# Modulation per row tile, its products in column groups, and a separate bank for the last half block

## Chip, cores and metric

The kernel runs on one core of a Trainium2 chip. The metric is the device time of one execution in microseconds (us). The engines are named as the profile names them: PE (TensorE) multiplies matrices, with PEld as its weight loads; DVE (VectorE), ACT (ScalarE) and POOL (GpSimd) work on elements; SP (SyncE) issues transfers.

## What is computed

One layer of a two-branch mixer over 256 latent and 256 context tokens, with 2048 features. The part that the change touches at the front is the modulation (`adaLN`) ahead of the input projection, and at the back the last normalisation:

```
shift, scale, gate = jnp.split(sc @ w_ada[l] + b_ada[l], 3, axis=-1)
hx = _rmsnorm(x, g_pre[l]) * (1.0 + scale[:, None]) + shift[:, None]
zx = hx @ w_in[l]
...
out = _rmsnorm(_mix_out(...), g_post[l])
x = x + gate[:, None] * out
```

The context stream does the same with `c_ctx`. `w_ada` is 2048 by 6144, and two thirds of it (32 MiB) are read for shift and scale. The rest of the layer (a depthwise convolution, a state space scan in both directions, a gated MLP, the output projection) is not changed.

## The kernel before

All weights are fp32. A weight piece is split into a rounded part `hi` (ACT) and a remainder `lo` (DVE), and every product of the projections is three matmuls, `hi` with `hhi`, `hi` with `hlo`, `lo` with `hhi`, where `hhi[k]` and `hlo[k]` are the two parts of the normalised and modulated input of feature tile k (lines 136 to 140).

**The first stage (lines 229 to 382)** walks the 16 feature tiles ("row tiles") as 16 rows. Row kt multiplies tile kt of the input with the part of the weights that belongs to it, `wst[kt]`: first the dt columns (`psdt`, lines 362 and 363, two matmuls), then seven column tiles psx0 to psx6, three matmuls each; psx3 and psx6 use 256 columns, the others 512. All sums stay in PSUM until row 15. In this stage the order on PE, DVE, ACT and POOL is the program's (`manual_schedule`, line 231), and `row_steps(kt)` writes out each row's steps.

Before row kt can run, its input tile must be shifted and scaled. The shift and scale come from `w_ada`, which arrives as 32 chunks of 1 MiB. `ada_mm(ci)` (line 205) multiplies one chunk: the two condition vectors are the weights (32 columns wide, two of them used), the chunk streams past, and four column groups of the array work side by side, each on another 32 feature columns. A unit is the accumulation that serves one or two tiles: units 0 and 1 serve tiles 0 and 1 (two chunks each, 64 columns per matmul), the seven others serve two tiles each (four chunks, 128 columns per matmul). When a unit is full, `ada_fin(u)` transposes it on DVE (line 222) and writes scale `ha` and shift `hb` with two ACT operations per tile (lines 224 and 226). Then `make_h(kt)` makes the tile: DVE scales it (line 307, two halves), ACT adds the shift and rounds to `hhi` (line 310, two halves), DVE makes `hlo` (line 312, two halves). `split_st(kt)` makes the weights' parts: ACT casts the whole row (line 299), DVE makes the dt remainder (line 300) and `lo` (line 301).

In rows 0 to 2 the two chunks stand apart, between products; in row 0 two more, chunks 4 and 5, stand at the end. In rows 3 to 13 the two chunks stand side by side. The tile of the next row is made in the middle of a row, once the unit that it needs is full: after chunk 3 for tile 1, after chunk 7 for tiles 2 and 3.

Transfers are issued on SP in program order: the input `xT` (4 MiB), then chunk 0, `wst[0]`, chunks 1 to 3, `wst[1]`, chunks 4 and 5, and in row kt chunks 2kt+6 and 2kt+7 and `wst[kt+2]`. Six chunks have room.

While PE waits for tile 0 it runs dummy matmuls (`warm`, line 254).

**The last stage (lines 1055 to 1149).** The output projection leaves eight banks, token tile tk = 0, 1 by column block b = 0 to 3. `ofinish` adds the last quarter of the sum. The last block (1, 3) is done as two halves of 256 columns in the same bank. For each block `o_sum` scales the bank and adds the other branch (DVE, line 1108), squares it with a row sum (ACT, line 1111), and multiplies by the gate (DVE, line 1114). Then per token tile: reduce, square root (ACT, line 1119), reciprocal (line 1122), and `o_out`: scale, add the input (DVE, line 1127) and send 256 KB out, on SP's and ACT's queues by turns. DVE's order is the program's here, the other engines' is the planner's.

Of the kernel before, what the change touches and what calls it, by code (L numbers as in the profile page):

```python
# [15 lines left out]
P = 128  # L16
D = 2048
# [8 lines left out]
WST = 64 + NST * P  # L26

# [14 lines left out]
def tile_hybrid_ssd_mlp(  # L42
# [252 lines left out]
    def split_st(kt):  # L295
        raw = wraw[kt]
        hi = wp["spl"].tile([P, WST + 64], F32R, tag="hi", name=f"hi_st{kt}")
        lo = wp["spl"].tile([P, WST - 64], F32R, tag="lo", name=f"lo_st{kt}")
        nc.scalar.copy(hi[:, 64:], raw)
        nc.vector.tensor_tensor(hi[:, 0:64], raw[:, 0:64], hi[:, 64:P].bitcast(F32), op=ALU.subtract)  # L300
        nc.vector.tensor_tensor(lo, raw[:, 64:], hi[:, P:].bitcast(F32), op=ALU.subtract)
        return hi, lo
# [20 lines left out]
    sp0 = {}  # L323

    def row_steps(kt):
# [3 lines left out]
        nxt = [("h", kt + 1), ("s", kt + 1)]  # L329
# [892 lines left out]
```

## Time and profile before

| | us |
|---|---|
| time, median of 3 runs (994.25 to 994.62) | 994.32 |
| the profiled execution's own time | 995.11 |
| its span | 993.4 |
| PE busy in the span | 976.1 |
| DVE busy | 623.0 |
| ACT busy | 493.6 |
| granted clock, mean share of full speed | 0.998 |

The page shows the span in 40 slices of 24.8 us. PE is at 9 tenths or more in all of them but the first and the last. The DMA engines are at 9 in the first four slices and between 1 and 8 after. Busy time on PE is modelled and consecutive matmuls overlap in it, so prices below are taken from one start to the next start, not from durations.

### The profile page before, as it was taken

The page shows a single profiled execution, that of the slowest core. Times are in us where ns is not written, and L with a number is a line of the kernel's source. Part 1 is how long each engine was busy: PE and PEld are TensorE (multiplying, and loading weights), DVE is VectorE, ACT ScalarE, POOL GpSimd, SP SyncE. Part 2 cuts the span into 40 slices and gives each one's busy share as a digit, 9 for nine tenths or more (in the row PEclk, how much of TensorE's full clock was granted, in tenths as well). Part 3 has the DMA queues.
Part 4 walks back from the last instruction along what each step waited for, and adds up shares of the span by engine and source line. Part 5 has one row for each costly group of instructions (what it writes and reads, how often), then busy time and mean ns, then how long its engine had stood idle before and what let it go on. Part 6 is the DMA issues. An engine that isn't in the chain of part 4 may idle for free.

```text
span 993.4 us, 14183 instructions
## 1 busy us (share of the span) xinstructions
PE 976.1 (98%) x5636; PEld 791.3 (80%) x5636; DVE 623.0 (63%) x944; ACT 493.6 (50%) x759; POOL 111.7 (11%) x162
## 2 busy tenths in 40 slices
PE   8999999999999999999999999999999999999996
PEld 3788888878787878787888878887888888888885
DVE  4345478877877666656667766666555564445636
ACT  4233348566655554545445334454565563346522
POOL 0000002423453221224000000000000000000000
PEclk9999999999999999999999999999999999999999
DMA  9999744233314324145778768774445445556722
GB/s 377 421 416 419 296 184 170 85 128 128 128 48 164 127 91 165 43 152 210 294 304 288 265 244 314 267 289 171 170 176 202 173 169 212 183 198 236 272 86 84
DMA packets 31554, 207.28 MB, mean 209 GB/s; under 512 B 4080, under 2 KB 4208, under 8 KB 7808
## 3 DMA queue, kind: packets, MB, share of 16 engines
q1 hardware_dynamic: 28656, 192.52, 51.3%
q0 software_dynamic: 2112, 12.65, 3.7%
q10 hardware_dynamic: 720, 1.20, 0.3%
q8 instruction: 44, 0.72, 0.3%
q14 instruction: 22, 0.18, 0.0%
HBM read 204.20 MB, written 2.16 MB: 208 GB/s over the span
## 4 chain that ended last, share of the span: by engine, by line
PE 80%; issue 8%; DMA 6%; DVE 2%; ACT 1%; POOL 1%; SPq 0%; DVEq 0%; POOLq 0%; ACTq 0%
PE psx L138 10%; PE psx L140 10%; PE psx L139 10%; PE pa L1027 8%; PE pa L1028 8%; PE pa L1029 8%; PE pm L1076 3%; PE pm L1075 3%; PE pm L1074 3%; PE psada L215 3%; PE pq L1075 2%; PE pq L1076 2%; PE pq L1074 2%; DMA ada<-in_wada_dram 2%; PE psc L697 1%
## 5 line engine op out<-in xcount | busy, mean ns | idle before, releaser
L82 DVE TENSOR_TENSOR lo_w<-w,hi_w 128x1024 fp32r<-128x1024 f32 x173 | 210.6, 1224 | 141.7 <-ACT hi_w L81 141.7
L81 ACT CAST hi_w<-w 128x1024 fp32r<-128x1024 f32 x173 | 182.0, 1052 | 203.6 <-PE pa L1029 132.2
L1027 PE MATMUL pa<-hi_w,hhi 128*128 128x512 f32 x512 | 202.3, 395 | 0.0
L1028 PE MATMUL pa<-lo_w,hhi 128*128 128x512 f32 x512 | 199.4, 390 | 0.8 <-DVE lo_w L82 0.8
L1029 PE MATMUL pa<-hi_w,hlo 128*128 128x512 f32 x512 | 199.5, 390 | 0.0
L138 PE MATMUL psx<-hhi,hi_w 128*128 128x512 f32 (+1 forms) x400 | 153.4, 383 | 0.0
L140 PE MATMUL psx<-hhi,lo_w 128*128 128x512 f32 (+1 forms) x400 | 145.9, 365 | 0.0
L139 PE MATMUL psx<-hlo,hi_w 128*128 128x512 f32 (+1 forms) x400 | 145.7, 364 | 0.0
L1027 PEld LDWEIGHTS pa<-hi_w,hhi 128*128 128x128 f32 x512 | 96.2, 188 | 20.7 <-issue 1.6
L1028 PEld LDWEIGHTS pa<-lo_w,hhi 128*128 128x128 f32 x512 | 96.2, 188 | 20.6 <-DVE lo_w L82 1.3
L1029 PEld LDWEIGHTS pa<-hi_w,hlo 128*128 128x128 f32 x512 | 96.1, 188 | 20.2
L495 DVE SCALAR_TENSOR_TENSOR xbc<-psx,pc,xbc 128x248 f32<-128x248 f32 (+1 forms) x204 | 83.5, 473 | 33.0 <-ACT xbc L479 32.0
L420 DVE TENSOR_TENSOR lo_w<-w,hi_w 128x1024 fp32r<-128x1024 f32 x61 | 79.4, 1308 | 23.9 <-ACT hi_w L414 23.8
L138 PEld LDWEIGHTS psx<-hhi,hi_w 128*128 128x128 f32 x400 | 75.5, 189 | 13.4 <-issue 2.9
L140 PEld LDWEIGHTS psx<-hhi,lo_w 128*128 128x128 f32 x400 | 75.4, 188 | 12.5
L139 PEld LDWEIGHTS psx<-hlo,hi_w 128*128 128x128 f32 x400 | 75.6, 189 | 12.2 <-issue 1.7
L414 ACT CAST hi_w<-w 128x1024 fp32r<-128x1024 f32 x61 | 63.5, 1044 | 26.0 <-PE psx L139 12.9
L885 DVE SCALAR_TENSOR_TENSOR junk<-gate,cb 128x2048 bf16<-128x2048 f32 x16 | 36.7, 2291 | 26.6 <-DMA gate<-in_wada_dram 26.5
L1074 PE MATMUL pm<-hi_w,hhi 128*128 128x512 f32 x128 | 50.0, 390 | 0.0
L1075 PE MATMUL pm<-lo_w,hhi 128*128 128x512 f32 x128 | 49.9, 390 | 0.0
L1076 PE MATMUL pm<-hi_w,hlo 128*128 128x512 f32 x128 | 49.6, 389 | 0.0
L138 PE MATMUL psx<-hhi,hi_st 128*128 128x512 f32 (+1 forms) x112 | 41.3, 368 | 0.0
(219 smaller groups left out, 1323.2 us busy)
## 6 DMA issues: line engine op xcount, KB each, us to landing
w<-in_wlat_dram SPq DMA_DIRECT2D x64, 1024.0 KB, 4.8
ada<-in_wada_dram SPq DMA_DIRECT2D x32, 1024.0 KB, 14.6
w<-in_wout_dram SPq DMA_DIRECT2D x32, 1024.0 KB, 4.8
w<-in_wxbc_dram SPq DMA_DIRECT2D x25, 1024.0 KB, 4.8
gate<-in_wada_dram SPq DMA_DIRECT2D x16, 1024.0 KB, 5.5
R<-acs POOLq DMA_DIRECT2D x8, 1024.0 KB, 5.4
wst<-in_wst_dram SPq DMA_DIRECT2D x16, 480.0 KB, 14.8
xT<-in_xch_dram SPq DMA_DIRECT2D x4, 1024.0 KB, 8.0
```

Of the source, the lines that this page charges most:

```text
L81: nc.scalar.copy(hi, raw)
L82: nc.vector.tensor_tensor(lo, raw, hi.bitcast(F32), op=ALU.subtract)
L138: nc.tensor.matmul(ps, lhsT=whi, rhs=hhi[k][:, s], start=start, stop=False)
L139: nc.tensor.matmul(ps, lhsT=whi, rhs=hlo[k][:, s], start=False, stop=False)
L140: nc.tensor.matmul(ps, lhsT=wlo, rhs=hhi[k][:, s], start=False, stop=stop)
L495: nc.vector.scalar_tensor_tensor(ao, zi, cw[:, k : k + 1], ao, op0=ALU.mult, op1=ALU.add)
L1027: nc.tensor.matmul(pa[tk], lhsT=hhi[k][:, t], rhs=whi[:, w], start=k == 0, stop=False)
L1028: nc.tensor.matmul(pa[tk], lhsT=hhi[k][:, t], rhs=wlo[:, w], start=False, stop=False)
L1029: nc.tensor.matmul(pa[tk], lhsT=hlo[k][:, t], rhs=whi[:, w], start=False, stop=k == KT - 1)
L1074: nc.tensor.matmul(p, lhsT=yh[:, t], rhs=whi[:, w], start=j == 0, stop=False)
L1075: nc.tensor.matmul(p, lhsT=yh[:, t], rhs=wlo[:, w], start=False, stop=False)
L1076: nc.tensor.matmul(p, lhsT=yl[:, t], rhs=whi[:, w], start=False, stop=hf == 0 and j == 15)
```

## The change

1. **Units.** Tiles 0 to 5 have a unit each (`NSING = 6`), the ten others are paired as before. Tile n is then shifted and scaled after chunks 2n and 2n+1 for n up to 5.
2. **Products of units 1 to 5** (`ada_rows`): one matmul of 256 columns for each of the eight feature tiles in a chunk, in place of 32 matmuls of 64 columns per chunk (units 0 and 1 of before) or 16 of 128 columns (its pairs). The four column groups take feature tiles by turns, so each holds a quarter of the sum for all 256 columns. Then DVE copies the bank's 256 columns to memory (`ada_keep`), two matmuls with a selector add the four groups and turn the result (`ada_sum`, two moving columns each, into the same bank), and ACT writes `ha` and `hb` straight from the bank (`ada_one`). Unit 0 and the pairs keep `ada_mm` and `ada_fin`.
3. **Order in the rows.** Rows 0 to 4 hold the two chunks of the next tile, apart from each other. Row 4 also holds chunk 12 ahead of psx6, row 5 chunks 13, 14, 15 apart, rows 6 and 7 their two chunks apart; from row 8 on the chunks stand side by side as before. The ACT cast of the next weights stands ahead of the tile's steps, the DVE `lo` after them.
4. **Loads.** `wst[0]` goes behind chunk 1 and is loaded and split in two pieces (448 and 512 columns); chunk 1 is loaded as two halves; up to row 3, `wst[kt+2]` goes ahead of the two chunks.
5. **The end.** The second half of block (1, 3) sums its last quarter in a bank of its own (`pr`, the place of block (0, 0)), so that the first half and what the bank already held of the second are read while PE still works. The last square root takes its second part directly, with the rest as bias. Of the last four blocks that go out, block 2 is made on PE (`px`): identity times input, started early, plus a diagonal of the reciprocal times the gated block; ACT copies and sends it. The three others stay on DVE and go out on SP.

```diff
-    UNITS = [(0,), (1,)] + [(m, m + 1) for m in range(2, KT, 2)]
+    UNITS = [(kt,) for kt in range(NSING)] + [(m, m + 1) for m in range(NSING, KT, 2)]
...
+    def ada_rows(c):
+
+        u, k0 = c // 2, 8 * (c % 2)
+        if k0 == 0:
+            ada_ps[u] = spt([P, 512], f"psada{u}")
+        ps = ada_ps[u]
+        raw = ada_raw.pop(c)
+        for kk in range(8):
+            g = kk % 4
+            nc.tensor.matmul(ps[32 * g : 32 * g + 32, 0:256], lhsT=sc[:, k0 + kk, :], rhs=raw[:, kk * 256 : (kk + 1) * 256],
+                             start=k0 == 0 and kk < 4, stop=k0 > 0 and kk >= 4)
+
+    def ada_keep(u):
+        cp = st2.tile([P, 256], F32, tag="cp", name=f"adac{u}")
+        nc.vector.tensor_copy(cp, ada_ps[u][:, 0:256])
+        ada_ps[u] = cp, ada_ps[u][:, 256:260]
+
+    def ada_sum(u):
+        cp, pt = ada_ps[u]
+        for q in range(2):
+            nc.tensor.matmul(pt[:, 2 * q : 2 * q + 2], lhsT=cp[:, q * P : (q + 1) * P], rhs=sel[:, 0, 0:2],
+                             start=True, stop=True)
...
     ada_load(0)
-    wst_load(0)
-    ada_load(1, 2, 3)
+    r1 = wp["raw"].tile([P, 2048], F32, tag="raw", name="ada_1")
+    for hf in range(2):
+        nc.sync.dma_start(r1[:, hf * 1024 : (hf + 1) * 1024], wada[1][:, hf * 1024 : (hf + 1) * 1024])
+    ada_raw[1] = r1
+    wraw[0] = st3.tile([P, WST], F32, tag="wst", name="wst0")
+    for a, b in ((0, WH), (WH, WST)):
+        nc.sync.dma_start(wraw[0][:, a:b], wst[0][:, a:b])
+    ada_load(2, 3)
     wst_load(1)
...
-        if kt == 0:
-            return m[:1] + [("a", 2)] + m[1:2] + [("a", 3)] + m[2:3] + [("f", 1)] + nxt + m[3:] + [("a", 4), ("a", 5)]
-        if kt < 3:
-            f = [("f", 2)] if kt == 1 else []
-            return m[:3] + [("a", 2 * kt + 4)] + m[3:5] + [("a", 2 * kt + 5)] + f + nxt + m[5:]
...
-        a = [("a", 2 * kt + 4), ("a", 2 * kt + 5)] if kt + 2 < KT else []
-        f = [("f", (kt + 1) // 2 + 1)] if kt % 2 else []
-        if kt < 5:
-            return m[:2] + a + f + nxt + m[2:]
-        return nxt[1:] + a + f + nxt[:1] + m
+        n = kt + 1
+        s_ = [("c", n), ("d", n), ("l", n)]
+        if n < NSING:
+            p6 = [("a", 2 * NSING)] if n == NSING - 1 else []
+            q = 4 if n == 1 else 3
+            return (m[:2] + [("r", 2 * n)] + m[2:q] + [("r", 2 * n + 1), ("c", n), ("k", n), ("d", n)] + m[q : q + 1]
+                    + [("g", n), ("o", n), ("h", n), ("l", n)] + m[q + 1 : 7] + p6 + m[7:])
+        a = [("a", c) for c in range(2 * kt + 4, 2 * kt + 6) if c < 2 * KT]
+        f = [("f", (kt + 1 - NSING) // 2 + NSING)] if kt % 2 else []
+        if n == NSING:
+            return m[:2] + [("a", 2 * kt + 3)] + m[2:3] + a[:1] + m[3:4] + s_ + a[1:] + f + [("h", n)] + m[4:]
+        if n < NSING + 3:
+            return m[:2] + s_ + a[:1] + m[2:4] + a[1:] + f + [("h", n)] + m[4:]
+        return s_ + a + f + [("h", n)] + m
...
+    px = spt([P, 512], "px")
+    nc.tensor.matmul(px, lhsT=ident, rhs=xf[1][:, 1024:1536], start=True, stop=False)
+    o_add(bk1[7], 1, 1536, 512)
+    o_sq(1, 3, 1536, 256)
+    o_gate(1, 1536, 256)
+    e1 = epso[:, 1:2]
+    nc.vector.tensor_reduce(ro[:, 1:2], oss[:, 1, 0:4], axis=mybir.AxisListType.X, op=ALU.add)
+    nc.vector.tensor_scalar(e1, ro[:, 1:2], 1.0 / D, EPS, op0=ALU.mult, op1=ALU.add)
+    o_add(pr, 1, 1792, 256)
+    o_sq(1, 4, 1792, 256)
+    o_gate(1, 1792, 256)
+    nc.scalar.activation(ro[:, 1:2], oss[:, 1, 4:5], AF.Sqrt, bias=e1, scale=1.0 / D)
     o_rec(1)
-    for b in range(4):
-        o_out(1, b)
+    dg = op1.tile([P, P], F32, name="dg")
+    nc.scalar.mul(dg, ident, ro[:, 1:2])
+    nc.tensor.matmul(px, lhsT=dg, rhs=ogs[1, 2], start=False, stop=True)
+    for b in (0, 1, 3):
+        o_out(1, b, nc.sync)
+    xb = xf[1][:, 1024:1536]
+    nc.scalar.copy(xb, px)
+    nc.scalar.dma_start(out[P : 2 * P, 1024:1536], xb)
```

## Rows read from the trace of the kernel before

**Rows 1.** Page, part 1: busy us (share of the span), instructions.

```profile
PE 976.1 (98%) x5636; PEld 791.3 (80%) x5636; DVE 623.0 (63%) x944; ACT 493.6 (50%) x759; POOL 111.7 (11%) x162
```

**Rows 2.** Timeline of PE, start of the stage: start us, us, instruction, idle before.

```profile
19.84 1.10 PE L215 MATMUL psada<-ada,sc 128*32 128x64 f32 x64 [1.31 <-DMA ada<-in_wada_dram]
...
23.25 0.49 PE L362 MATMUL psdt<-hhi,hi_st 128*128 128x512 f32 x1 [0.39 <-ACT hhi L310]
23.77 0.49 PE L363 MATMUL psdt<-hlo,hi_st 128*128 128x512 f32 x1
```

**Rows 3.** Busy time by windows: the DMA engines' rate (last column, GB/s).

```profile
15.00:20.00 5.00, 3.69 (x89) 1.86 (x92) 2.82 (x7) 1.15 (x2) 0.00 (x0) 1.00 1.00 418
```

**Rows 4.** Timeline of DVE and ACT, the making of tile 0.

```profile
21.00 0.25 DVE L222 STREAM_TRANSPOSE adat<-psada 128x64 f32<-128x64 f32 x1 [0.53 <-PE psada L215]
21.29 0.39 ACT L224 ACTIVATE ha<-adat,bsc,pc 128x2 f32<-128x2 f32 x1 [2.60 <-DVE adat L222]
21.71 0.88 DVE L307 SCALAR_TENSOR_TENSOR xT<-xT,ha,y 128x256 f32<-128x256 f32 x2 [0.46 <-ACT ha L224]
22.29 0.91 ACT L310 ACTIVATE hhi<-xT,hb 128x256 fp32r<-128x256 f32 x2 [0.43 <-DVE xT L307]
22.83 0.88 DVE L312 SCALAR_TENSOR_TENSOR hlo<-xT,hb,hhi 128x256 fp32r<-128x256 f32 x2 [0.24 <-ACT hhi L310]
```

**Rows 5.** Timeline of PE, rows 1 to 4: chunk 5, tile 2's wait, row starts.

```profile
32.43 1.08 PE L215 MATMUL psada<-ada,sc 128*32 128x128 f32 x32 [0.54 <-DMA ada<-in_wada_dram]
...
42.36 0.50 PE L362 MATMUL psdt<-hhi,hi_st 128*128 128x512 f32 x1 [1.58 <-DVE hi_st L300]
...
43.40 0.47 PE L140 MATMUL psx<-hhi,lo_st 128*128 128x512 f32 x1
...
47.76 0.50 PE L138 MATMUL psx<-hhi,hi_st 128*128 128x512 f32 x1
...
49.61 0.40 PE L362 MATMUL psdt<-hhi,hi_st 128*128 128x512 f32 x1
...
56.36 0.50 PE L362 MATMUL psdt<-hhi,hi_st 128*128 128x512 f32 x1
```

**Rows 6.** Timeline of PE: four products of 64 columns between tile products.

```profile
130.34 1.00 PE L320 MATMUL pstok<-y 128*128 128x64 f32 x8
131.15 0.48 PE L138 MATMUL psx<-hhi,hi_st 128*128 128x512 f32 x1
```

**Rows 7.** Timeline of PE: one product in each of four groups, 512 columns.

```profile
10.65 1.06 PE L268 MATMUL pss<-y,ones 128*32 128x512 f32 x8
11.65 1.13 PE L256 MATMUL psw<-ones 128*128 128x512 f32 x2
```

**Rows 8.** Timeline: one fp32 product of few columns and ACT reading it.

```profile
17.10 0.40 PE L276 MATMUL psb<-y,sel 128*128 128x16 f32 x2
17.53 0.27 ACT L279 ACTIVATE rc<-psb,epsc 128x16 f32<-128x16 f32 x1 [2.68 <-PE psb L276]
```

**Rows 9.** Timeline of DVE, the remainder of the weights of row 2.

```profile
42.22 1.09 DVE L301 TENSOR_TENSOR lo_st<-wst,hi_st 128x896 fp32r<-128x896 f32 x1
```

**Rows 10.** Timeline of DVE and ACT, the last two half blocks and the end.

```profile
984.39 0.48 DVE L1108 SCALAR_TENSOR_TENSOR ob<-pq,rr,ob 128x256 f32<-128x256 f32 x1 [1.39 <-PE pq L1086]
985.25 0.48 DVE L1108 SCALAR_TENSOR_TENSOR ob<-pq,rr,ob 128x256 f32<-128x256 f32 x1
986.55 0.29 ACT L1119 ACTIVATE ro<-ro,epso 128x1 f32<-128x1 f32 x1 [0.22 <-DVE ro L1118]
986.88 0.16 DVE L1122 RECIPROCAL ro<-ro 128x1 f32<-128x1 f32 x1 [0.36 <-ACT ro L1119]
987.08 2.74 DVE L1127 SCALAR_TENSOR_TENSOR xf<-og,ro,xf 128x512 f32<-128x512 f32 x4
```

**Rows 11.** Busy time by windows at the end: PE, PEld, DVE, ACT, POOL, granted clock, DMA.

```profile
984.00:987.00 3.00, 0.35 (x3) 0.14 (x2) 2.01 (x6) 1.31 (x5) 0.00 (x0) 1.00 0.00 0
...
990.00:991.00 1.00, 0.00 (x0) 0.00 (x0) 0.00 (x0) 0.00 (x0) 0.00 (x0) 0.50 1.05 365
```

More of the change, by code (lines that the diff above doesn't have):

```diff
@@ L292, in tile_hybrid_ssd_mlp, with split_hi, split_dt, split_lo @@
     psx[3] = psx[3][:, 0:256]
[L295 to L302, printed above, removed]
+    sp0 = {}
+    def split_hi(kt, a=0, b=WST):
+        if a == 0:
+            sp0[kt] = (wp["spl"].tile([P, WST + 64], F32R, tag="hi", name=f"hi_st{kt}"),
+                       wp["spl"].tile([P, WST - 64], F32R, tag="lo", name=f"lo_st{kt}"))
+        nc.scalar.copy(sp0[kt][0][:, 64 + a : 64 + b], wraw[kt][:, a:b])
+    def split_dt(kt):
+        hi = sp0[kt][0]
+        nc.vector.tensor_tensor(hi[:, 0:64], wraw[kt][:, 0:64], hi[:, 64:P].bitcast(F32), op=ALU.subtract)
+    def split_lo(kt, a=64, b=WST):
+        hi, lo = sp0[kt]
+        nc.vector.tensor_tensor(lo[:, a - 64 : b - 64], wraw[kt][:, a:b], hi[:, 64 + a : 64 + b].bitcast(F32), op=ALU.subtract)
     def make_h(kt):
@@ L1095, in tile_hybrid_ssd_mlp @@
     oproj(1, bk1, [o for o in plain if o[0] < 12])
-    parts = [(tk, b, 0, 512) for tk in range(2) for b in range(4)][:-1] + [(1, 3, 0, 256), (1, 3, 256, 256)]
-    for part in parts:
-        ofinish(*part)
+    for b in range(4):
+        ofinish(0, b)
     xf = [load_raw(xtok[tk], f"xf{tk}") for tk in range(2)]
-    epso = op1.tile([P, 1], F32, name="epso")
+    epso = op1.tile([P, 2], F32, name="epso")
     nc.vector.memset(epso, EPS)
@@ L1127, in o_out @@
         nc.vector.scalar_tensor_tensor(xb, ogs[tk, b], ro[:, tk : tk + 1], xb, op0=ALU.mult, op1=ALU.add)
[L1128 removed]
+        q.dma_start(out[tk * P : (tk + 1) * P, cs], xb)
     man = ExitStack()
@@ L1133, in tile_hybrid_ssd_mlp @@
         o_sum(0, b)
-    o_rms(0)
+    pr = acp.tile([P, 512], F32, tag="acc", name="pr")[:, 0:256]
+    for b in range(3):
+        ofinish(1, b)
+    ofinish(1, 3, 0, 256)
+    ofinish(1, 3, 256, 256, pr)
+    nc.vector.tensor_reduce(ro[:, 0:1], oss[:, 0, :], axis=mybir.AxisListType.X, op=ALU.add)
+    nc.scalar.activation(ro[:, 0:1], ro[:, 0:1], AF.Sqrt, bias=epso[:, 0:1], scale=1.0 / D)
     o_rec(0)
     for b in range(3):
-        o_out(0, b)
+        o_out(0, b, nc.scalar if b % 2 else nc.sync)
         if b == 0:
             o_sum(1, 0)
-    o_out(0, 3)
+    o_out(0, 3, nc.scalar)
     o_sum(1, 1)
     o_sum(1, 2)
-    o_sum(1, 3, 0, 256)
-    o_sum(1, 3, 256, 256)
-    o_rms(1)
-    o_rec(1)
-    for b in range(4):
-        o_out(1, b)
+    px = spt([P, 512], "px")
[10 more added lines that the diff above has]
+    nc.scalar.activation(ro[:, 1:2], oss[:, 1, 4:5], AF.Sqrt, bias=e1, scale=1.0 / D)
+    o_rec(1)
+    dg = op1.tile([P, P], F32, name="dg")
[6 more added lines that the diff above has]
+    nc.scalar.dma_start(out[P : 2 * P, 1024:1536], xb)
     man.close()
```

84 lines of the change are left out of this document (46 added, 38 removed).

## The prediction

> **What bounds the kernel now.** I read the page's busy times first: PE is busy for 976.1 us of the span [rows 1], so nothing that merely shortens another engine's work moves the end. What counts is work added to PE or taken from it, the few places where PE waits, and the end, where PE has stopped. Then I read PE's timeline for its waits. In the first stage there are four: 1.31 us for chunk 1 and 0.39 us for tile 0 [rows 2], 0.54 us for chunk 5 and 1.58 us for tile 2 [rows 5]. After 42.36 us the rows follow each other at 7.25 us (row 2, chunks apart) and 6.75 us (row 3, chunks together) with no wait shown [rows 5]. So in this stage the change can win at most some 3.8 us by removing waits, and everything that it adds to PE, or newly makes PE wait for, is paid in full: the later stages are as busy and give nothing back. The profiled execution's span is 993.4 us, its own time 995.11; it lies 0.8 above the median of 994.32. I work out differences in the trace and add them to the median.
>
> **The start.** `wst[0]` moves behind chunk 1. It is 480 KB, and at 418 GB/s [rows 3] that is 1.2 us, nearly all of the 1.31 us wait for chunk 1 [rows 2]; with the half loads the rest goes too. Tile 0's chain is unchanged (transpose 21.00, scale 21.29, `psdt` 23.25 [rows 2, 4]); the first piece of `wst[0]` lands about 0.6 us behind chunk 1, and its cast of 448 columns fits ahead of the scale. So row 0 starts 1.3 us earlier, near 21.95: -1.3, with 0.9 to 1.4 as bounds (the pieces' rows are short, and no row shows such a load). Row 0 then meets two small waits. Its first tile product ends near 23.4; chunk 2 is next. Its landing has no row, but chunk 5 lands at 32.4 [rows 5], and the 3.47 MiB between them take 8.7 us at 418 GB/s, so 23.7: +0.3. The new copy of unit 1 on DVE starts after chunk 3, and only the short psx3 (0.35) covers it; a 256-column read of PSUM takes 0.48 [rows 10]: +0.1. Together +0.4.
>
> **Waits that go.** Tile 2 no longer needs chunks 6 and 7, and chunk 5 is wanted a row later: -0.54 and -1.58, -2.1 in all.
>
> **Work added to PE.** Five selector products. The trace of before has none of two columns; four products of 64 columns take 0.81 [rows 6], so a pair 0.40, with the switch back to tile products up to 0.56; I take 0.44, five times: +2.2. The chunks themselves stay alike: one with 512 columns per matmul and group, the same columns in all, takes 1.00 from start to next start [rows 7], against 1.03 for chunk 1, which starts at 19.84 and whose transpose follows at 21.00 [rows 2, 4]: 0, with 0.5 either way for ten chunks. Standing apart costs more than standing together: row 2 took 0.50 us longer than row 3 [rows 5]; I take off 0.2 for its restart after the wait and for `lo` being just late at 43.40, and have 0.3 for each pair that is split. Before, rows 3 to 7 hold five pairs and row 0 a sixth (chunks 4 and 5); after, chunks 2 to 19 all stand apart. +1.8, with 0 and 3.0 as bounds.
>
> **New waits.** In rows 1 to 3 the tile of the next row now begins only after the selector products, late in the row. Let those start at time 0. One such product reaches ACT after 0.43 [rows 8], the second 0.20 later; ACT to DVE 0.42, DVE to the first half of `hhi` 0.58, from there to `psdt` 0.96 [rows 2, 4]: tile ready for the first dt matmul at 2.6. `hlo` starts 1.12 after the scaling and is usable 0.94 after that [rows 2, 4]: second dt matmul at 3.1. `lo` is queued on DVE behind `hlo`; it starts 0.85 after it and its first reader starts 1.18 later [rows 5, 9]: third matmul of psx0 at 4.2. PE meanwhile has the products (0.44), psx3 (0.35) and psx4 to psx6 (1.85, from 47.76 to 49.61 [rows 5]): it is there at 2.65, just in time for the first, 0.2 early for the second, then 0.4 early for the third. Queued behind these waits is the whole row. So 0.6 for each of tiles 2, 3 and 4. For tile 1 psx3 lies ahead of the products instead, and PE is 0.3 early for the first as well: 1.0. Tile 5 has chunk 12 behind its products (1.2 us): covered. Tile 6 is made after chunk 15 by the old chain: transpose to second dt matmul 2.8 us [rows 2, 4], from 0.13 after the chunk, against 2.2 us of products and 0.23: 0.5. Sum +3.3. Bounds: 0, if PE reaches these points later than I think, and 5 if the chain from the bank is 0.3 longer in each. From row 8 on the order has the chunks ahead of the row and hides the chain as before.
>
> **Loads later on.** After row 2 each row asks for 2.47 MiB in over 7 us and the engines bring it in 6.2 us at 418 GB/s, so the earlier `wst` and the later chunks cost nothing; without that cover a late chunk would cost what chunk 5 costs now, 0.54.
>
> **The end.** Now the first half's add waits until 984.39, for the whole bank; the second half's follows at 985.25, the reciprocal at 986.88, and four scalings take 2.74 from 987.08 [rows 10]. After, DVE starts on the first half up to 1.39 earlier, right behind its previous block; add of 512 columns, multiply, reduce and one more small step bring the second half's add to 984.8. From there to the reciprocal it is 1.63 less the reduce (0.2): 986.2 to 986.4. DVE has three scalings left at 0.66 each and issues the last at 988.5, against 989.85. The fourth block: diagonal on ACT 0.4, fp32 product 1.13 [rows 7], copy some 0.65: sent at 988.7. -1.15. Bounds: -1.5 if the PE branch is hidden, 0 if the reads still wait for PE.
>
> The Trainium skill, "TensorE: Matmul & The Clock Gate", Part 1, says that TensorE left idle falls to the lower clock, which speaks against a product placed after the engine has run dry. The trace has the granted clock at full (2.4 GHz) from 984 to 987 with PE's last matmul in it, and at half (1.2 GHz) from 990 to 991 [rows 11]. My product falls near 987 and the early identity product lies between, so I take the full clock; the half clock is a rival below.
>
> **The sum.** -1.3 + 0.4 - 2.1 + 2.2 + 1.8 + 3.3 - 1.15 = +3.15; 994.32 + 3.15 = 997.5.
>
> **Rivals.**
> 1. *Rows at PE's pace.* The tile chain is quicker or PE slower between the products and the next row, by 0.6 us per row, and no new wait shows. For it: the first dt matmul is already just in time. Against: `hlo` and `lo` stand one behind the other on DVE, and these prices are measured. -3.3: 994.2.
> 2. *Faster.* Besides that, splitting pairs costs nothing, because row 2's extra 0.50 was all restart. It decides at a row period: if rows 1 to 3 run at 7.2 us or less with the products in them, this holds. 994.2 - 1.8 = 992.4, or 992.0 with the end's best case. The Trainium skill, "TensorEngine Tiling (Array Packing)", Key Properties, speaks against it: a change of tiling mode drains the engine, so each chunk set apart pays twice. Here that is 0.3 per pair by the rows, and I kept it.
> 3. *The half clock at the end.* The product then takes about 0.85 longer and the gain falls to 0.3: 998.4.
> 4. *The column groups don't overlap with 256 columns.* Ten chunks at up to four times their stream of 0.9: some 27 us more. The 512-column case overlaps [rows 7], so this is nearly excluded.
>
> **Numbers.** Forecast 997.5 with 0.50, rival 1 0.25, rival 2 0.14, rival 3 0.09, rival 4 0.02. 0.2% is 2 us, about what a measurement of this kernel can tell from no change. Slower (above 996.3): forecast and rivals 3 and 4, less 0.07 for a forecast that is half right, 0.54. Same: rival 1 and what of the forecast falls there, 0.32. Faster: rival 2, 0.14. Range: from rival 2's edge, 992.5, to 999.3, the forecast with the upper bounds of products and half of those of waits; outside lie rivals 2 and 4.
>
> **What would show it.** Right: row 0 starting near 22.0 and row 2 near 39, rows 1 to 3 some 8 us long, PE waits for `hhi` or `hlo` at the two dt matmuls and for `lo` at the third matmul of psx0, each 0.2 to 0.4, and row 8's chunk some 4 us later than now; the second half's add near 984.8 plus that shift. Wrong: row periods near 7.3, no DVE wait on PE in rows 1 to 4, or a fold product far from 0.22 each; at the end, a copy of `px` that ends after the last DVE scaling by over 0.5 us.

## Result and the profile after

| | before | after |
|---|---|---|
| time, median of 6 runs each, us | 994.47 | 998.00 (997.75 to 999.78) |
| ratio | | 1.0038, 95% interval 1.0026 to 1.0051 |
| the profiled execution's own time, us | 995.11 | 998.10 |
| its span, us | 993.4 | 996.4 |

The changed kernel is slower by 0.26% to 0.51%, beyond the 0.2% that a measurement can tell from no change. The forecast was 997.5, slower.

In the first and last stage line numbers have moved: `psdt` is L408 and L409, the three matmuls of a psx tile L141 to L143, the 256-column chunk products L219, the old chunk products L249, the selector products L230. The page's first part answers [rows 1]:

```profile
PE 984.7 (99%) x5436; PEld 788.5 (79%) x5436; DVE 622.9 (63%) x947; ACT 494.0 (50%) x762; POOL 111.7 (11%) x162
```

PE is busier by 8.6 us although the span grew by 3.0 and 200 instructions are gone. Durations overlap in that number, so it says where to look, not how much. The timeline of PE in the first stage (start, us, instruction, idle before) answers [rows 2, 5]; a line without brackets can still hide a wait, which shows when the step from one start to the next is longer than usual. An fp32 product of the program stands there as two matmuls, so a chunk of eight products is x16:

```profile
22.08 0.51 PE L408 MATMUL psdt<-hhi,hi_st 128*128 128x512 f32 x1 [0.39 <-ACT hhi L358]
...
23.40 0.40 PE L143 MATMUL psx<-hhi,lo_st 128*128 128x512 f32 x1
23.93 1.07 PE L219 MATMUL psada<-ada,sc 128*32 128x256 f32 x16
...
36.35 0.50 PE L230 MATMUL psada<-sel,adac 128*128 128x2 f32 x4
36.71 0.37 PE L141 MATMUL psx<-hhi,hi_st 128*128 128x256 f32 x1
36.92 0.28 PE L142 MATMUL psx<-hlo,hi_st 128*128 128x256 f32 x1
...
38.88 0.45 PE L408 MATMUL psdt<-hhi,hi_st 128*128 128x512 f32 x1
39.34 0.50 PE L409 MATMUL psdt<-hlo,hi_st 128*128 128x512 f32 x1
39.68 0.39 PE L141 MATMUL psx<-hhi,hi_st 128*128 128x512 f32 x1
39.90 0.39 PE L142 MATMUL psx<-hlo,hi_st 128*128 128x512 f32 x1
40.34 0.49 PE L143 MATMUL psx<-hhi,lo_st 128*128 128x512 f32 x1
40.77 1.07 PE L219 MATMUL psada<-ada,sc 128*32 128x256 f32 x16
41.77 0.50 PE L141 MATMUL psx<-hhi,hi_st 128*128 128x512 f32 x1
...
72.98 0.49 PE L408 MATMUL psdt<-hhi,hi_st 128*128 128x512 f32 x1
73.50 0.50 PE L409 MATMUL psdt<-hlo,hi_st 128*128 128x512 f32 x1
...
89.43 0.50 PE L408 MATMUL psdt<-hhi,hi_st 128*128 128x512 f32 x1
```

The same views of the kernel before have the start of row 8 and the last matmul of the output projection:

```profile
85.46 0.50 PE L362 MATMUL psdt<-hhi,hi_st 128*128 128x512 f32 x1
...
984.07 0.28 PE L1086 MATMUL pq<-hhi,yal 128*128 128x256 f32 x1
```

Row 0 starts at 22.08 (before 23.25 [rows 2]), row 2 at 38.88 (before 42.36 [rows 5]): so far the kernel leads by 3.5 us. Then rows 2 and 3 take 8.1 each, where they took 7.25 and 6.75. Rows 4 to 7 take 9.33, 8.54, 7.43 and 9.02, where they took 8.90, 6.73, 6.73 and 6.74 (the 9.02 holds four chunks: row 7's own two and the two that now stand ahead of row 8). Row 8 starts at 89.43, where it started at 85.46 before: 3.97 behind. From there to the end of the projections little changes: PE's last matmul of the output projection starts at 987.95 and ends 0.28 later, 3.88 after the one of before (984.35).

From 38.88 on one sees the two new waits. From the first to the second dt matmul it is 0.46 instead of 0.23; to the third matmul of psx0 0.44 instead of 0.23. The waits of PEld, the weight load that a waiting matmul needs first, name what ended them (engine, tile, line, waited for: us, times, longest):

```profile
PEld psdt L409 <- DVE hlo L360: 2.0, 6, 0.3
PEld psx L143 <- DVE lo_st L350: 1.9, 4, 0.5
PEld psdt L408 <- ACT hhi L358: 1.8, 3, 1.2
```

The `hlo` of six tiles and the `lo` of four: these are tiles 0 to 4 and 6, and tiles 1 to 4. Tile 0 waited so before, too [rows 2]. The end answers [rows 10]; first DVE, then PE, then the windows (PE, PEld, DVE, ACT, POOL, granted clock, DMA share, GB/s):

```profile
986.83 0.75 DVE L1159 SCALAR_TENSOR_TENSOR ob<-pq,rr,ob 128x512 f32<-128x512 f32 x1
...
988.48 0.47 DVE L1159 SCALAR_TENSOR_TENSOR ob<-pr,rr,ob 128x256 f32<-128x256 f32 x1
...
989.92 0.16 DVE L1177 RECIPROCAL ro<-ro 128x1 f32<-128x1 f32 x1 [0.51 <-ACT ro L1216]
990.11 2.08 DVE L1182 SCALAR_TENSOR_TENSOR xf<-og,ro,xf 128x512 f32<-128x512 f32 x3
```

```profile
987.95 0.28 PE L1139 MATMUL pr<-hhi,yal 128*128 128x256 f32 x1
988.07 1.02 PE L1206 MATMUL px<-xf,ident 128*128 128x512 f32 x2
990.57 1.12 PE L1220 MATMUL px<-og,dg 128*128 128x512 f32 x2 [1.48 <-ACT dg L1219]
```

```profile
990.00:992.00 2.00, 1.12 (x2) 0.30 (x2) 1.96 (x4) 0.67 (x2) 0.00 (x0) 1.00 0.14 54
992.00:994.00 2.00, 0.00 (x0) 0.00 (x0) 0.19 (x1) 0.32 (x1) 0.00 (x0) 0.85 1.03 378
```

The first half is added while PE still works (986.83). The reciprocal comes 1.69 us after the end of PE's last matmul of the output projection, against 2.53 before. The product with the diagonal runs at the full granted clock. From that last matmul to the end of the span it is 8.16 us, against 9.05; "PE's last matmul" below is always this one, measured at its end.

### The profile page after: what moved, and what is told of

Same layout as the page of the kernel before. It is cut to its first block, busy times and chain, and to the rows that moved or that the text cites. A ratio compares the mean times of both kernels' runs of the same rounds, so it can differ in the third digit from the quotient of the medians.

```text
span 996.4 us, 13797 instructions
## 1 busy us (share of the span) xinstructions
PE 984.7 (99%) x5436; PEld 788.5 (79%) x5436; DVE 622.9 (63%) x947; ACT 494.0 (50%) x762; POOL 111.7 (11%) x162
## 4 chain that ended last, share of the span: by engine, by line
PE 75%; issue 10%; DMA 7%; DVE 5%; ACT 2%; POOL 1%; SPq 0%; DVEq 0%; ACTq 0%; POOLq 0%
PE psx L141 10%; PE psx L143 10%; PE psx L142 10%; PE pa L1079 5%; PE pa L1081 5%; PE pa L1080 5%; DMA gate<-in_wada_dram 5%; PE pm L1128 3%; PE pm L1127 3%; PE pm L1126 3%; PE pq L1127 2%; PE pq L1128 2%; PE pq L1126 2%; DVE lo_w L85 2%; PE psada L249 2%
## 5 line engine op out<-in xcount | busy, mean ns | idle before, releaser
L141 PE MATMUL psx<-hhi,hi_w 128*128 128x512 f32 (+1 forms) x400 | 153.4, 383 | 0.0
L143 PE MATMUL psx<-hhi,lo_w 128*128 128x512 f32 (+1 forms) x400 | 145.9, 365 | 0.0
L141 PEld LDWEIGHTS psx<-hhi,hi_w 128*128 128x128 f32 x400 | 75.5, 189 | 13.3 <-issue 2.9
L143 PEld LDWEIGHTS psx<-hhi,lo_w 128*128 128x128 f32 x400 | 75.4, 189 | 12.6
L141 PE MATMUL psx<-hhi,hi_st 128*128 128x512 f32 (+1 forms) x112 | 42.8, 382 | 0.0
```

The costliest lines, as they stand in the source:

```text
L141: nc.tensor.matmul(ps, lhsT=whi, rhs=hhi[k][:, s], start=start, stop=False)
L143: nc.tensor.matmul(ps, lhsT=wlo, rhs=hhi[k][:, s], start=False, stop=stop)
```

## Experiments

Times are medians, ratios those to the kernel before on the same chip (993.8 to 994.0 us there). The later stages vary: the MLP's products `pa` take 372.4 to 373.5 us, from the first start to the last end, in one execution or another of these kernels. So a step of the first stage is read from row starts of one trace, and only the sum from the median.

### The new end alone

The kernel before with part 5 of the change.

```diff
+    pr = acp.tile([P, 512], F32, tag="acc", name="pr")[:, 0:256]
...
-    parts = [(tk, b, 0, 512) for tk in range(2) for b in range(4)][:-1] + [(1, 3, 0, 256), (1, 3, 256, 256)]
...
+    ofinish(1, 3, 0, 256)
+    ofinish(1, 3, 256, 256, pr)
```

> The kernel before with the new end alone (bank of its own for the last half block, the fourth block through PE); the first stage is the old one. Theory (first stage costs 3.9 us, the end gives back about 0.8): from PE's last projection matmul to the end of the span it takes 8.2 us instead of 9.05 (after: 996.4 less 988.2), so 993.5, 0.8 to 1.1 below before. Rival (the end gives nothing, and the first stage costs the whole 3.5): 994.4, no difference from before.

993.07 us, ratio 0.9992 (0.9984 to 1.0001); from PE's last matmul to the end of the span 8.21 us. The end is worth 0.84 us by the traces (9.05 to 8.21) and 0.94 by the medians, whose interval just includes no change. So the front costs some 4.5 by the medians, and 3.9 to 4.0 by the traces.

This kernel has the old loads, and its trace is the second one that shows their start: chunk 0 at 16.95, then a wait for chunk 1, and row 0 at 22.93.

```profile
19.52 1.10 PE L215 MATMUL psada<-ada,sc 128*32 128x64 f32 x64 [1.46 <-DMA ada<-in_wada_dram]
```

### The last block on DVE again

```diff
-    px = spt([P, 512], "px")
-    nc.tensor.matmul(px, lhsT=ident, rhs=xf[1][:, 1024:1536], start=True, stop=False)
...
-    for b in (0, 1, 3):
-        o_out(1, b, nc.sync)
-    xb = xf[1][:, 1024:1536]
-    nc.scalar.copy(xb, px)
-    nc.scalar.dma_start(out[P : 2 * P, 1024:1536], xb)
+    for b in range(4):
+        o_out(1, b, nc.scalar if b % 2 else nc.sync)
```

> The changed kernel with the fourth of the last blocks back on DVE (no identity product, no diagonal, no copy; blocks sent on the two queues by turns, as before), with the bank of its own and the split square root kept. Theory 1 (the PE branch gives nothing: its transfer was issued at 992.35, 0.13 behind another one, and took 2.96 to land where transfers 0.66 apart take 2.4): DVE sends the fourth block 0.66 later than the third, at 992.88, and it lands at 995.3 as now; from PE's last projection matmul to the end of the span 8.2 as now; 998.0. Rival (the branch saves the whole 0.66 of a scaling): 8.8, 998.6.

998.26 us, ratio 1.0043 (1.0029 to 1.0056), and 8.08 us from PE's last matmul to the end, against 8.16. DVE does four scalings:

```profile
990.22 2.74 DVE L1182 SCALAR_TENSOR_TENSOR xf<-og,ro,xf 128x512 f32<-128x512 f32 x4
```

Counted from PE's last matmul, the last transfer is issued at 4.66, where the changed kernel issues it at 4.12, and lands at 7.05, where the other landed at 7.08. So the branch over PE gains nothing. In both traces the four transfers of 256 KB land 0.66 to 0.76 us apart, at 378 GB/s (256 KB take 0.69 at that rate); the one that was issued 0.13 behind another took 3.0 us to land, the others 2.3 to 2.4:

```profile
out_dram<-xf SPq DMA_DIRECT2D x3, 256.0 KB, 2.3
out_dram<-xf ACTq DMA_DIRECT2D x1, 256.0 KB, 3.0
```

(the issues of the changed kernel: queue, count, size, median us to landing). Before, they landed 0.70 to 0.80 apart, with the first issued at 987.86. The first is issued 3.51 us after PE's last matmul before, 2.67 after: -0.84, which is nearly the whole gain of 0.88.

### The first block in two halves

A test of that reading: an earlier first issue, and nothing else.

```diff
-    for b in (0, 1, 3):
+    for c0 in (0, 256):
+        o_out(1, 0, nc.sync, c0, 256)
+    for b in (1, 3):
         o_out(1, b, nc.sync)
```

> The changed kernel, with the first of the last four output blocks scaled and sent as two halves of 256 columns, so that its first transfer is issued some .25 us earlier and the last ones some .1 to .2 us later. Theory (the end is the first issue and then four transfers of 256 KB at the rate of the DMA engines, .66 to .76 us each, one behind the other; when the last is issued doesn't count): from PE's last matmul of the output projection to the end of the span some 7.9 us, against 8.16 in the changed kernel. Rival (the last issue decides, as the prediction had priced it): 8.2 to 8.4 us. Either is below what the median can show; the median should stay near 998 us.

997.55 us, ratio 1.0040 (1.0026 to 1.0053); 8.03 us from PE's last matmul (start 987.54) to the end, against 8.16. The first issue is 0.26 earlier, and half of that arrives: from the first issue to the last landing it is now 4.59 us, not 4.41. The last issues stand no earlier than in the changed kernel (4.12 after PE's last matmul in both), so it isn't they that set the end. The direction is the theory's, the size half of it, and why the other half is lost isn't shown. The step is small, but larger than the spread: the ten traces with the new end as it is take 8.08 to 8.21 for this stretch, the two with halves (this one and the last combination below) 8.03 and 8.01. The 8.08 of the kernel without the branch over PE lies at the edge of that spread.

### `lo` ahead of the tile's steps

```diff
-                    [("r", 2 * n + 1), ("c", n), ("k", n), ("d", n)] + m[q : q + 1]
-                    + [("g", n), ("o", n), ("h", n), ("l", n)] + ...
+                    [("r", 2 * n + 1), ("c", n), ("k", n), ("d", n), ("l", n)] + m[q : q + 1]
+                    + [("g", n), ("o", n), ("h", n)] + ...
```

> The changed kernel with one step moved: in rows 0 to 4 DVE makes the remainder lo of the next weights right after the dt remainder, ahead of the tile's steps, not behind them. Theory (the third matmul of psx0 waits for lo only because lo is queued behind hlo): in rows 2 to 4 the wait of 0.2 and the slower matmul after it (0.1) go, DVE has the 1.0 us free while PE works on the selector products; in row 1 it shifts the tile by 0.3 and wins nothing. -0.9 to -1.2, about 997.0, row period 7.8 instead of 8.1. Rival (PE meets the same delay at the next step, or DVE is late with the tile): row period stays 8.1, 998.0 or above.

997.30 us, ratio 1.0033 (1.0021 to 1.0046). Rows 1 to 4 take 7.88, 7.82, 7.82 and 9.02 us (8.17, 8.11, 8.12 and 9.33 in the changed kernel): 0.3 less each, row 1 too, where the expectation saw nothing to win. The rows tell the two kernels apart; the intervals of the ratios overlap. In PE's timeline the third matmul of psx0 now follows at once, and the `hlo` wait at the second dt matmul stays (39.53 to 39.98):

```profile
39.53 0.43 PE L408 MATMUL psdt<-hhi,hi_st 128*128 128x512 f32 x1
39.98 0.50 PE L409 MATMUL psdt<-hlo,hi_st 128*128 128x512 f32 x1
...
40.56 0.40 PE L142 MATMUL psx<-hlo,hi_st 128*128 128x512 f32 x1
40.79 0.40 PE L143 MATMUL psx<-hhi,lo_st 128*128 128x512 f32 x1
41.12 1.07 PE L219 MATMUL psada<-ada,sc 128*32 128x256 f32 x16
```

A wait thus costs its length and 0.1 more at the next step: 0.21 + 0.10 for `lo`. The `lo` wait was time on the path, not cover for something else.

### Chunks of rows 5 to 7 side by side

```diff
-            return m[:2] + [("a", 2 * kt + 3)] + m[2:3] + a[:1] + m[3:4] + s_ + a[1:] + f + [("h", n)] + m[4:]
+            return m[:2] + s_ + [("a", 2 * kt + 3)] + a + f + [("h", n)] + m[2:]
         if n < NSING + 3:
-            return m[:2] + s_ + a[:1] + m[2:4] + a[1:] + f + [("h", n)] + m[4:]
+            return m[:2] + s_ + a + f + [("h", n)] + m[2:]
```

> The changed kernel with the chunks of rows 5, 6 and 7 side by side right behind psx0 and the tile's steps there, as rows 3 and 4 of before have it; rows 0 to 4 as changed. Theory (a chunk that stands apart costs 0.15 more than one beside another, and tile 6 is late because it is made late in row 5): four joints of 0.3 go (-1.2) and the waits of 0.5 at the start of row 6 go: -1.7, 996.3. Rival (splitting is free): -0.5, 997.5.

996.20 us, ratio 1.0022 (1.0012 to 1.0032). Rows 5, 6 and 7 take 7.62, 6.71 and 8.69 us instead of 8.54, 7.43 and 9.02: 1.97 less.

```profile
66.22 0.40 PE L143 MATMUL psx<-hhi,lo_st 128*128 128x512 f32 x1
66.55 2.83 PE L249 MATMUL psada<-ada,sc 128*32 128x128 f32 x96
...
72.91 0.40 PE L408 MATMUL psdt<-hhi,hi_st 128*128 128x512 f32 x1
73.15 0.40 PE L409 MATMUL psdt<-hlo,hi_st 128*128 128x512 f32 x1
```

Row 7, where only the place of two chunks differs, gives the price of one pair split: 0.33. Three chunks apart are two splits (row 5), two are one (row 6): four splits, 1.3 us. The other 0.64 is tile 6's wait: 0.25 at the first dt matmul, 0.29 at the second and 0.10 behind it in the changed kernel (72.98, 73.50), and none here (72.91, 73.15).

### The selector products twice

```diff
-        for q in range(2):
+        for q in (0, 1, 0, 1):
```

> The changed kernel, with the selector products of units 1 to 5 done twice (the second result replaces the first; the output is the same). It measures what these products cost by themselves. Theory (TensorE's work on the path, paid in full): five times some .42 us as read in the changed kernel's trace, so 998.0 + 2.1 = about 1000.1 us, row periods near 8.5 instead of 8.1, and the waits for hlo and lo behind them as long as before. Rival (the products lie in time in which TensorE would wait for the next tile's hlo and lo anyway, .23 and .21 us a row): the waits shrink by as much as the products grow, near 998.0 to 998.5 us.

999.69 us, ratio 1.0059 (1.0047 to 1.0072). Rows 1 to 3 take 8.63, 8.55 and 8.57: 0.45 more than in the changed kernel. The `hlo` and `lo` waits have their old length.

```profile
36.90 0.95 PE L230 MATMUL psada<-sel,adac 128*128 128x2 f32 x8
37.71 0.36 PE L141 MATMUL psx<-hhi,hi_st 128*128 128x256 f32 x1
```

Each pair costs 0.45 in full. That the waits don't shrink proves less than the expectation made of it: the tile's chain begins behind the last of these products, so doubling them moves the chain as well.

### The old products for single tiles

Units and order stay as changed, but the chunks of units 1 to 5 are multiplied in pieces of 64 columns and turned on DVE, as units 0 and 1 were before.

```diff
-                    ... [("r", 2 * n + 1), ("c", n), ("k", n), ("d", n)] + m[q : q + 1]
-                    + [("g", n), ("o", n), ("h", n), ("l", n)] ...
+                    ... [("r", 2 * n + 1), ("c", n), ("f", n), ("d", n)] + m[q : q + 1]
+                    + [("h", n), ("l", n)] ...
...
-             ... "r": ada_rows
+             ... "r": ada_mm
```

> The changed kernel, but units 1 to 5 use the old products (64 columns, four column groups over feature columns) and the DVE transpose: no copy of the bank, no selector products; order of the rows as in the changed kernel. Theory (the selector products are paid in full on PE, and the tile starts later behind them): five times 0.45 go, chunks cost 0.03 more each (+0.3), the tile starts some 1.0 earlier against PE, so the waits for hhi and hlo in rows 2 to 4 go and of the lo wait 0.1 to 0.2 stays: -2.2 + 0.3 - 1.2 = -3.1, 994.9. Rival 1 (only the products count, the waits have another cause): -1.9, 996.1. Rival 2 (products hidden): no change, 998.0.

1002.20 us, ratio 1.0072 (1.0058 to 1.0086): all three expected times missed. Where PE doesn't stop, the theory holds: row 2 begins without the `hlo` and `lo` waits, and row 4 takes 8.30 us instead of 9.33, which is the selector products (0.45) and the two waits (0.65) but for 0.07. But rows 2 and 3 take 11.45 and 10.86 us. In the middle of chunk 7, with its data there, PE stood still; the windows show the granted clock of that time, the DMA engines and their rate:

```profile
42.23 0.98 PE L249 MATMUL psada<-ada,sc 128*32 128x64 f32 x53
45.85 0.41 PE L249 MATMUL psada<-ada,sc 128*32 128x64 f32 x11 [2.64 <-issue]
```

```profile
40.00:45.00 5.00, 3.21 (x122) 2.24 (x121) 0.00 (x0) 0.99 (x1) 0.00 (x0) 1.00 1.01 414
45.00:50.00 5.00, 4.15 (x24) 3.35 (x24) 3.11 (x7) 2.37 (x5) 0.00 (x0) 0.74 1.02 422
```

"issue" means that the profile shows nothing that PE waited for. A second stop of 1.76 us stands in chunk 9 (until 56.23). After each the clock is reduced for a while, which adds to the price.

### Short pieces in the new products

What stopped PE there? The kernels differ in the number of PE instructions: a chunk has 64 matmuls in the trace, and as many weight loads, in that form, 16 of each in the changed kernel. Here the changed kernel's products keep their form and work, but half of each chunk is cut into pieces of 32 columns: 36 matmuls where there were 8 in the program.

```diff
-        for kk in range(8):
-            g = kk % 4
-            nc.tensor.matmul(ps[32 * g : 32 * g + 32, 0:256], ...
+        for k4 in (0, 4):
+            n = 256 if (k0, k4) in ((0, 0), (8, 4)) else 32
+            for c0 in range(0, 256, n):
+                for g in range(4):
+                    kk = k4 + g
+                    nc.tensor.matmul(ps[32 * g : 32 * g + 32, c0 : c0 + n], ...
```

> The changed kernel, but in units 1 to 5 half of each chunk's matmuls of 256 columns are cut into eight of 32 columns: the same columns in all, 36 matmuls per chunk where there are 8 (64 columns throughout: 32). Theory from the run with the old products, where PE stood still for 2.6 and 1.8 us in the middle of chunks 7 and 9 with no releaser shown (PE runs out of instructions while the transfers fill the engines): standstills of 1.5 to 3 us come back in rows 2 to 4, row periods there of 10 to 11 us at least once, +4 us or more, 1002. Rival (the standstill belonged to the old layout of the chunks, not to the number of instructions): only the shorter matmuls' own price, up to 0.3 per chunk: up to 1001, all rows 2 to 4 alike and no standstill over 0.5 us.

1006.58 us, ratio 1.0122 (1.0108 to 1.0135), with the same kind of stop, in chunk 5 and once more in chunk 11, and the granted clock at half after the first. The second window is that ahead of the second stop:

```profile
39.15 1.28 PE L222 MATMUL psada<-ada,sc 128*32 128x32 f32 x23 [3.45 <-issue]
...
67.83 0.78 PE L222 MATMUL psada<-ada,sc 128*32 128x32 f32 x26 [0.88 <-issue]
```

```profile
40.00:45.00 5.00, 5.00 (x19) 3.98 (x15) 2.24 (x7) 1.85 (x5) 0.00 (x0) 0.50 1.02 419
...
65.00:67.00 2.00, 1.96 (x108) 1.39 (x94) 0.00 (x0) 0.00 (x0) 0.00 (x0) 1.00 0.34 135
```

The traces also record the transfers that bring instructions, 16 KB each. In the two kernels with stops, seven begin between 20 and 66 us, in the changed kernel four (in the kernel before six, and its trace shows no such stop). All four stops end 2.4 to 2.6 us after one of them began: 45.85 after 43.28, 56.23 after 53.75, 39.15 after 36.61, 67.83 after 65.40. So does a fifth, of 0.37 us, in row 1 of the kernel with the old products (38.70 after 36.13). The two longest are those in which the transfer began only when PE already stood (43.28 after 43.21, 36.61 after 35.70). I read this as PE running out of instructions and waiting for the next block. That more short matmuls bring the stops is shown; that the block is what ends them rests on these five times. Full DMA engines aren't needed for it: around the first three stops they moved 412 to 419 GB/s, but while the block ahead of the fourth was under way (65.40 to 66.33) they were a third busy, at 135 GB/s, and that stop too ended 2.43 us after the block began. Whether a full DMA stage makes a block start late isn't shown. The Trainium skill, "Runtime: NRT & Kernel Launch", Instruction fetch mechanics, says that an engine's instructions come in blocks of 16 KiB that the sequencer fetches by DMA while it works through the last one, mostly hidden. The blocks agree with the trace; that they are hidden doesn't hold for these five.

### `wst[0]` ahead of chunk 1 again

```diff
     ada_load(0)
+    wraw[0] = st3.tile([P, WST], F32, tag="wst", name="wst0")
+    for a, b in ((0, WH), (WH, WST)):
+        nc.sync.dma_start(wraw[0][:, a:b], wst[0][:, a:b])
...
-    wraw[0] = st3.tile([P, WST], F32, tag="wst", name="wst0")
-    for a, b in ((0, WH), (WH, WST)):
-        nc.sync.dma_start(wraw[0][:, a:b], wst[0][:, a:b])
     ada_load(2, 3)
```

> The changed kernel with the first weights (two pieces, as changed) loaded ahead of chunk 1 again, behind chunk 0. Theory of the prediction (chunk 1's landing sets the start, and the move is worth 1.2): row 0 starts 1.2 later than with the move, chunk 2 then no longer makes PE wait (0.2 to 0.3): 0.9 slower, 998.9. Rival, from the runs so far (in two of four executions with the move, the norm products ran at nearly half their pace until 12 or 13 us and row 0 started at 23.1 to 23.2, near the 23.25 of before; the move then buys nothing): 0 to 0.3 slower, 998.0 to 998.3, row 0 starting at 23.2 to 23.6.

998.64 us, ratio 1.0046 (1.0034 to 1.0059): 0.6 above the changed kernel, between what theory and rival expected, and the intervals of the two kernels overlap. The trace can't say more, since in it something else made row 0 late. PE's timeline from the dummies to row 0:

```profile
9.37 2.08 PE L297 MATMUL psw<-ones 128*128 128x512 f32 x2
...
13.01 1.13 PE L297 MATMUL psw<-ones 128*128 128x512 f32 x2
...
18.80 1.99 PE L249 MATMUL psada<-ada,sc 128*32 128x64 f32 x128
...
23.11 0.50 PE L408 MATMUL psdt<-hhi,hi_st 128*128 128x512 f32 x1 [0.39 <-ACT hhi L358]
```

Two dummies take 2.08 at first and 1.13 from 13 us on, so chunk 0 begins at 18.80 and finds chunk 1 already there. This slow beginning is no mark of a kernel: it lasts to about 13 us in three traces of these experiments, whose rows 0 start at 23.1 to 23.2, with `wst[0]` ahead of chunk 1 (23.11) or behind it (23.10 and 23.24). In the others it ends between 8 and 11. Of these, the nine with the new loads start row 0 between 21.8 and 22.3, the two with the old loads at 23.25 and 22.93, both behind a wait for chunk 1 (1.31 and 1.46 us). So the new loads are worth 0.6 to 1.5 us after a quick beginning; after a slow one the order makes no difference here.

### Combinations

Row by row the experiments suggest a kernel: the new end and loads; single units only for tiles 0 to 3, of which 0 and 1 with the old products, so that two pairs of selector products are left; the chunks side by side from row 1 on; `lo` first.

```diff
-NSING = 6
+NSING = 4
...
+        if kt < 3:
+            p = [("a", 8)] if kt == 2 else []
+            return (m[:2] + [("r", 2 * n), ("r", 2 * n + 1), ("c", n), ("k", n), ("d", n), ("l", n)] + m[2:3]
+                    + [("g", n), ("o", n), ("h", n)] + m[3:7] + p + m[7:])
```

> New end and new loads; units of one tile for tiles 0 to 3 only, with the new products and selectors for tiles 2 and 3 alone (0 and 1 have the old ones), pairs from tile 4 on; chunks side by side from row 1 on (chunk 8 alone), lo made ahead of the tile's steps in rows 1 and 2. Theory (the sum of the terms as the rows gave them): against the kernel before -0.5 for chunk 5's wait, -1.7 for tile 2's, +0.9 for two pairs of selector products, -0.45 for chunks side by side, +0.5 for a short wait at row 1, -0.9 for the end, 0 to -1.2 for the start: -2.1 to -3.3, so 990.8 to 992.1, about 991.5, below both kernels. Rival (the selectors' rows bring new waits of 0.6 each, and chunk 11 is late): 993.3.

992.96 us, ratio 0.9991 (0.9982 to 1.0000), short of the expected 990.8 to 992.1. Row 8 starts at 85.16, only 0.3 ahead of the kernel before. A new wait had come, for the weights of chunk 11:

```profile
51.14 1.08 PE L249 MATMUL psada<-ada,sc 128*32 128x128 f32 x32 [1.13 <-DMA ada<-in_wada_dram]
```

The next kernel puts three psx tiles between chunks 10 and 11 and between 12 and 13, and makes tile 1 earlier in row 0.

```diff
-            return m[:2] + [("a", 9)] + a + f + s_[:1] + [("h", n)] + s_[1:] + m[2:]
+            return m[:2] + [("a", 9)] + a[:1] + s_ + m[2:5] + a[1:] + f + [("h", n)] + m[5:]
+        if kt == 4:
+            return m[:2] + a[:1] + s_ + [("h", n)] + m[2:5] + a[1:] + m[5:]
```

> v_mix with two things moved. Row 0: the chunk that fills the wait for tile 1 comes one matmul group later and tile 1's steps run between the chunk's copies, so that row 1 should wait less for hhi (.42 us in v_mix), hlo and lo (.3 and .4). Row 3 and row 4: the two chunks of a pair stand apart, with three projection groups between, so that the wait for chunk 11's weights (1.13 us in v_mix at 51.14) has work ahead of it. Theory (both waits are idle time of TensorE that other work can cover): row 4 starts near 54.6 instead of 56.17, and the time is near 991.4 us (990.8 to 992.4). Rival (the weights land when they land, and the next pair waits for what this one waited for): row 4 earlier but row 5 as in v_mix, near 992.9 us.

992.73 us, ratio 0.9991 (0.9981 to 1.0000), again short of what was expected. Row 4 starts at 54.88 instead of 56.17, as the theory had it, but row 5 at 64.35 instead of 64.96: half of the gain is given back, because tile 4 now comes too late for its first dt matmul and a pair is split.

```profile
54.88 0.50 PE L422 MATMUL psdt<-hhi,hi_st 128*128 128x512 f32 x1 [0.43 <-ACT hhi L366]
```

With the first block of the end in two halves as well:

> v_mix2 with the first of the last four output blocks sent in two halves. Theory as above: some .25 us less than v_mix2, near 992.5 us; from PE's last matmul to the end of the span 7.9 to 8.0. Rival: as v_mix2 or .1 more, near 992.8 us.

992.40 us, ratio 0.9988 (0.9979 to 0.9997); 8.01 us from PE's last matmul to the end, 8.17 in the combination above. It has the lowest median of the kernels here. The changed kernel is clearly behind it; against the kernel before the interval just excludes no change, but 0.12% is less than the 0.2% named above, so a gain over it isn't shown.

## Why the prediction was right

The sign, the size (+3.15 against +3.0 in span and +3.5 in medians) and the place were right. That the sum came so near is in part luck: by the traces the first stage cost 0.3 less than forecast and the end gave 0.3 less, and the two nearly cancel. By its steps; a step is measured from one start to the next, less the same step where nothing waits:

| step | predicted | measured |
|---|---|---|
| start of row 0 | -1.3 | -1.17 |
| row 0's small waits: chunk 2, copy of unit 1 | +0.4 | +0.20 and +0.16 |
| waits that go: chunk 5, tile 2 | -2.1 | -0.6 and -1.9 |
| selector products | +2.2 | +2.4 |
| chunk products of another shape | 0 | -0.1 |
| six pairs split | +1.8 | 6 x 0.31 = +1.9 |
| new waits: tile 1; tiles 2 to 4; tile 5; tile 6 | +1.0; 3 x 0.6; 0; +0.5 | +0.95; 3 x 0.65; 0; +0.64 |
| sum up to row 8 | +4.3 | +3.97 by row 8 itself |
| the end | -1.15 | -0.88 |

The measured terms add up to 4.3 before rounding, 0.3 more than the row shows. The starts of before have that much: with its wait the pair of chunks 4 and 5 took 2.63 where a pair in row 3 takes 1.88, which is 0.14 more than the 0.6 in the table, and row 4 began with 0.14 of waiting and had its `lo` 0.06 late, waits that the prediction didn't see.

- *The start.* Right in this trace, but the step took for granted that chunk 0 begins when it did in the one trace of before. The beginning varies by 1 us from execution to execution. Where it is slow, chunk 1 is there in time either way: row 0 starts at 23.11 with the weights ahead of it, and at 23.10 and 23.24 with them behind. So the start gains nothing in one execution and 0.6 to 1.5 us in another, and the -1.17 is that of two quick ones. The difference between 3.0 and 3.5 has another source: the profiled execution of before lay 0.6 above its median, that of after 0.1.
- *Waits that go.* 0.4 too small: the idle time in brackets counts from the modelled end of the matmul before, and a stop makes the next step late too. Tile 2's 1.58 [rows 5] was 1.74 by starts, with 0.18 more in the steps behind.
- *Selector products and splits.* From the nearest rows [rows 5, 6], and confirmed to 0.01 and 0.03 by the kernels that double the products and that join the chunks. Row 2's extra 0.50 over row 3 was rightly divided into 0.2 and 0.3; rival 2 took all of it for restart. Of the 0.31, 0.20 lie in the steps into and out of a chunk (0.33 each where 0.23 is usual), and the rest is that two chunks side by side take 1.88 and two apart 2.00. The rule that the Trainium skill, "TensorEngine Tiling (Array Packing)", Key Properties, gives on a change of tiling mode agrees with these 0.31 to 0.33; no run here separates the drain from the rest.
- *New waits.* Named with engine, tile and place, and each within 0.15. For tiles 2 to 4 the two parts were 0.34 for `hlo` and 0.31 for `lo`, where the prediction had 0.2 and 0.4; the 0.85 from `hlo` to `lo`, which the rows that it names don't show, was 0.80. The chain from bank to tile, put together from single rows of tile 0 [rows 4, 8, 9], was long enough to decide: 8.1 us a row, where rival 1 would have shown some 7.5 and rival 2 7.2 or less. Taking the `lo` wait away gave back 0.3 a row, and with the old products, where no stop stood, both waits went.
- *The end.* The mechanism was right up to the reciprocal, which came even earlier: 986.04 after taking off the shift of 3.88, against 986.2 to 986.4. The step that failed is the last: the term went by the last issue (988.5 on DVE, 988.7 over PE). The last issue, 0.54 later in the kernel without the branch over PE, made the end no later (8.08 against 8.16), so that branch is worth nothing. What fits all traces better is the first issue and four transfers at the engines' rate behind it: 0.84, not 1.15. The kernel with halves bears this out only by half.
- *Rivals.* 1 and 2 fell by the row periods. 3 fell: the product at 990.57 ran at a granted clock of 1.00 (2.4 GHz), 1.5 us after the identity product ended; the clock sank only later, in 992 to 994 (0.85). The Trainium skill, "TensorE: Matmul & The Clock Gate", Part 1, spoke for it with the rule that an idle TensorE falls to the lower clock; the trace agrees only for the time behind this product. 4 fell: a chunk takes 1.00 from start to next start (40.77 to 41.77).
- *The range.* Its upper end, 999.3, doesn't follow from the bounds that it names: selector products (+0.6), chunks (+0.5) and split pairs (+1.2) at their upper bounds, with half of that of the waits (+0.85), make some 1000.7. The measured 998.0 lies inside either.

What the prediction didn't see is why the single units are affordable at all. With the products of before the kernel takes 3.4 us more by the ratios and 4.2 by the medians, through stops of which no row of before shows the price.

## What to carry to other kernels

Removing a wait for data by making that data in smaller portions pays only if the portion's own chain (copy, product, two engines) still ends before the row that needs it; write the chain down step by step from rows of the trace, and count splits and restarts. Where an output leaves in equal pieces at the full DMA rate, look at the first issue before the last: here the last one 0.54 us later cost nothing, and the first one 0.26 earlier gave 0.13. And many short matmuls can have a price beyond their columns: here they made PE stand still, for 0.4 to 3.5 us a stop.

## What the runs showed of the hardware

- PE stood still in the middle of an accumulation, with its data there: stops of 2.64, 1.76, 3.45 and 0.88 us, each ending 2.4 to 2.6 us after a 16 KB instruction transfer had begun. The DMA engines moved 412 to 419 GB/s around the first three, and 135 while the transfer ahead of the fourth was under way. The granted clock was 0.74 and 0.50 in the windows behind the two longest.
- Identical products ran at nearly half pace (2.08 for two dummies, then 1.13) up to 8 to 13 us, for a time that differs from execution to execution. The column of the granted clock shows 1.00 there.
- A transfer of 256 KB that was issued 0.13 us behind another took 3.0 us to land, the others 2.3 to 2.4.
